# A two-layer sequence trunk on one core: the first MLP's down projection as seven block products, and sums of the last row group on GpSimd

## The chip, the core and the metric

One core of one Trainium2 chip. A core has TensorE (PE, matrix products and the transposes made with them), VectorE (DVE), ScalarE (ACT), GpSimd (POOL) and SyncE (SP, which here only issues transfers). The five have instruction streams of their own and wait for each other through semaphores. The metric is the device time of one execution in microseconds (us); lower is better. All tensors are fp32.

## The reference

```python
def reference(x, mem, ...):                  # x (1, 512, 1024), mem (1, 256, 1024)
    h = x
    for layer in range(2):
        # layer 0: gated DeltaNet mixer; layer 1: Conformer convolution module
        h = h + mixer(rms_norm(h, ...), ...)
        h = h + memory_cross_attention(rms_norm(h, ...), ...)
        h = h + sq_relu_mlp(rms_norm(h, ...), w_up, w_down)
    return rms_norm(h, final_norm)

def sq_relu_mlp(h, w_up, w_down):            # 512x1024 @ 1024x4096, then @ 4096x1024
    return jnp.square(jax.nn.relu(h @ w_up)) @ w_down

def conformer_conv(h, ...):
    u = h @ w_pw1 + b_pw1
    u = u[..., :1024] * jax.nn.sigmoid(u[..., 1024:])
    c = causal_depthwise_conv(u, w_dw) + b_dw          # 31 taps
    return jax.nn.silu(layer_norm(c, ln_g, ln_b)) @ w_pw2 + b_pw2
```

The change concerns the MLP of layer 0. Behind it in the program comes the convolution module of layer 1.

## The kernel before, in words

**Layout and precision.** Activations lie feature-major: a tile holds 128 features by 512 tokens, and the residual `h` is eight such tiles. Each value is split into a rounded part and a rest (`xh` and `xl`, `uh` and `ul`; for weights `wh` and `wl`), and each product is made as three matmuls, high by high, low by high and high by low (`mm3`, L282 to L288). `proj` (L294) runs `mm3` over the eight 128-row pieces k of a contraction of 1024: 24 matmuls of 128x512 for one output tile.

**Weights.** They stream in 128x1024 tiles, in an order planned ahead (`order`, `need`). `wload` (L222) issues a tile's transfer on SP's queue into one of six `raw` buffers; `wsplit` makes `wh` from it (ACT cast, L245) and `wl` (DVE subtraction, recorded at the helper line L69), with three buffers each; `wnext` (L258) hands them to the matmuls in the planned order and keeps loads and splits a few tiles ahead.

**Normalization.** An RMS norm's statistics are collected while its inputs are made. For each finished `h` tile `Norm.add` issues `xh` (ACT L372), `xl` (DVE L72) and a square (ACT L379), and adds the squares up (GpSimd, the last sum on DVE). `Norm.stat`, placed inside the matmuls that consume the tiles, splits the sum (`sqh`, `sql`), sums it over the partitions with matmuls, and takes a root (ACT) and a reciprocal (`rb`, DVE L395). The factor `rb` is multiplied in later, when a product is read out of PSUM.

**The MLP of layer 0** (`mlp`) has four groups of 1024 hidden rows. In the order up 0, up 1, down 0, up 2, down 1, up 3, down 2, down 3 it makes per group eight up tiles and eight down tiles of 24 matmuls each. A down tile is added to the residual by one DVE instruction `h<-dn,h`. In down 3 this instruction also reorders the tokens by phase (t mod 4), as the convolution wants them, and calls `add` of the convolution's norm tile by tile. Ahead of down 3 some work for later is issued (`mid`): the norm of the memory for layer 1's attention (eight `ml` instructions) and loads of the convolution's taps.

**The MLP of layer 1** (`mlp7`) multiplies the 512x1024 activations of a group by its 1024x1024 down weights in the Strassen-Winograd way: seven products of blocks, half the size in each direction, instead of eight (`ORDER7`). Here the activations stand in PE and the weights stream, so the output is token-major. A product is 2 row halves c x 2 weight halves h x 2 k x 3 = 24 matmuls of 512 columns. Sums of weight blocks are needed (T1 to T4): they are made in memory by transfers that add to their destination (`more`, L233, on GpSimd's queue). T1, T2 and T4 are made one after the other in the same two `t` tiles, each after the last use of the one before. The products are collected in `acc` tiles: four for the output blocks (n, m), and `m` and `b` for parts that enter several blocks, each for two row halves c. In the last group `m` and `b` are joined to the blocks by DVE instructions `acc<-acc,acc`, and `final` makes the closing RMS norm out of the token-major rows. At group 0, `turn` transposes the residual into the first four `acc` pairs.

**Behind the first MLP** comes the convolution module. Its first projection (`pw_mm`) makes sixteen tiles in pairs m, one of the value half (`pa`) and one of the gate half (`sg`). The two tiles of the pair m=0 are made one after the other: all eight k of the first, then all of the second, with `norm.stat` inside the second tile's k=1. The taps of the convolution are done by DVE (`ca<-x,prm,ca`, L1192) and partly by GpSimd (`ca<-ca,cvp`), beside the matmuls.

Of the kernel before, what the change touches and what calls it, by code (L numbers as in the profile page):

```python
# [8 lines left out]
F32 = mybir.dt.float32  # L9
F32R = mybir.dt.float32r  # L10
# [27 lines left out]
def tile_trunk(ctx, tc, xT, memT, x_d, mem_d, prm_d, adt_d, bdw_d, tap_d, fin_d, w_ab, w_kq, w_v, w_z, w_dno, w_pw1, w_pw2,  # L38
# [141 lines left out]
    def plan_mlp7(layer):  # L180
        for g in range(4):
            for i in range(4):
                plan(("up", layer, g * 4 + i), w_up[layer, g * 4 + i])
            n, base7["u", g] = len(loads), len(order)
# [4 lines left out]
            for u in range(14):  # L189
                order.append((("dn7", g), u))  # L190
# [12 lines left out]
    plan_mlp(0)  # L203
# [31 lines left out]
    def wsplit():  # L235
# [5 lines left out]
        raw = combos7(1, i, hf) if kind == "dn7" else ws["raw"].pop(need[u])  # L241
# [13 lines left out]
        if kind == "dn7":  # L255
            after7(1, i, hf)
# [13 lines left out]
    def combos7(layer, g, u):  # L270
# [3 lines left out]
        t = ws["raw"].pop(need[u + base7["u", g]])  # L274
# [781 lines left out]
    def mlp(layer, norm, hres, nxt, mid):  # L1056
        xs = norm.xs
        hid = {}
        cur = list(hres)
        st = {"first": []}  # L1060

        def up_ev(g, i, ps):
# [4 lines left out]
            hid.setdefault(g, []).append(split(u, "u"))  # L1067

        for kind, g in MLP_ORDER:
            if (kind, g) == ("dn", 3):  # L1070
                mid()
            for i in range(8):
                w = wnext((kind, layer, g * 4 + i // 2), i % 2)
                ps = psum(kind)
                if kind == "up":
                    proj(w, xs, ps, inside={1: norm.stat} if (g, i) == (0, 1) else None)
                    if g == 0 and i < 2:
                        st["first"].append(ps)
                        if i == 1:
                            for j in range(2):  # L1080
                                up_ev(0, j, st["first"][j])
                    else:
                        up_ev(g, i, ps)
                else:
                    proj(w, hid[g], ps)
                    hn = slot(s="h")
                    if g == 3:
                        tt(dve, by_phase(hn), phased(ps), phased(cur[i]), ALU.add)
                        nxt.add(i, hn)
                    else:  # L1090
                        tt(dve, hn, ps, cur[i], ALU.add)
                    cur[i] = hn
        return cur

# [7 lines left out]
    def by_phase(t):  # L1102
        return t.rearrange("p (s t) -> p s t", s=4)

# [10 lines left out]
    def conformer(norm, hres, nxt):  # L1115
# [409 lines left out]
    h = mlp(0, n2, h, n3, lambda: (mem_gain(1, 0), mem_gain(1, 1), taps(NTAP)))  # L1525
# [5 lines left out]

    def mlp7(layer, norm, hres):
        xs = norm.xs
        acc, first = {}, []
        gt = []

        def turn(i):
            n, m, c = i // 4, i // 2 % 2, i % 2
            ps, a = psum("hT"), slot(s="acc")
            for j in range(4):  # L1540
# [295 lines left out]
```

## Time and profile before

| | |
|---|---|
| time, median of 3 runs | 1486.36 us (1484.01 to 1486.58) |
| the profiled execution: time / span | 1487.96 us / 1486.0 us |
| mean granted TensorE clock | 0.997 of full speed |
| busy: PE, DVE, ACT, POOL | 99%, 66%, 49%, 16% of the span |

Stages of the span, from the timeline: the MLP of layer 0 from 562.70 to 823.80 us, the convolution module from there to 994 us with memory projections and layer 1's cross-attention behind it, the MLP of layer 1 from 1192.81 us to the end.

How to read the profile: an instruction is named by its line, engine, operation and `out<-in` of the program's names. A matmul's duration overlaps the next one's, so that matmuls are counted and priced by the busy time of a stretch. In a timeline row the first number is the start in us from the span's start, the second the duration, and a bracket at the end says how long the engine had been idle before it and what ended that.

### The profile page before, as it was taken

The numbers are of one execution on the slowest core, as the hardware profiler recorded it, in microseconds if no ns is written. First come the engines' busy times: TensorE is split into PE (matmuls) and PEld (weight loads), VectorE is DVE, ScalarE is ACT, GpSimd is POOL, SyncE is SP. The second block draws the span as 40 slices with busy tenths as digits, with TensorE's granted clock in tenths as the row PEclk, the third lists the DMA queues.
The fourth block names the chain that finished last, engine by engine and source line by source line (L and its number), as shares of the span: only waits on it lengthen the run. The fifth ranks groups of instructions, "written<-read, shape, count | busy, mean of one in ns | idle before, by whom it ended". The sixth has DMA issues, their size and how long they took to land.

```text
span 1486.0 us, 19375 instructions
## 1 busy us (share of the span) xinstructions
PE 1472.0 (99%) x7362; PEld 1241.1 (84%) x7362; DVE 986.7 (66%) x1468; ACT 729.0 (49%) x1262; POOL 240.2 (16%) x255
## 2 busy tenths in 40 slices
PE   9999999999999999999999999999999999999997
PEld 7888889988888888888888889988888888888885
DVE  5889888867555543443436699984645766767677
ACT  6766865655444432332314555464444554434344
POOL 1411310103112000000002388302112000000000
PEclk9999999999999999999999999999999999999999
DMA  7232123432213332223224524652203467575634
GB/s 269 93 114 72 58 87 126 142 115 97 73 34 109 99 100 95 91 98 100 99 99 156 174 96 135 192 178 93 86 29 113 114 170 178 140 193 140 186 99 113
DMA packets 55821, 176.63 MB, mean 119 GB/s; under 512 B 6961, under 2 KB 9265, under 8 KB 55729
## 3 DMA queue, kind: packets, MB, share of 16 engines
q1 hardware_dynamic: 50688, 158.10, 32.0%
q0 software_dynamic: 4608, 16.78, 6.6%
q8 instruction: 58, 0.95, 0.3%
q10 hardware_dynamic: 432, 0.52, 0.1%
q14 instruction: 35, 0.28, 0.1%
HBM read 172.49 MB, written 2.10 MB: 117 GB/s over the span
## 4 chain that ended last, share of the span: by engine, by line
PE 94%; DVE 3%; ACT 2%; issue 1%; DMA 1%; POOL 0%; SPq 0%; DVEq 0%
PE up L288 8%; PE up L287 8%; PE up L286 8%; PE dn L287 4%; PE dn L288 4%; PE dn L286 4%; PE dn L1578 3%; PE dn L1579 3%; PE dn L1577 3%; PE pw L288 3%; PE pw L287 3%; PE pw L286 3%; PE h L286 3%; PE h L287 2%; PE h L288 2%; PE xo L287 2%
## 5 line engine op out<-in xcount | busy, mean ns | idle before, releaser
L245 ACT CAST wh<-raw 128x1024 fp32r<-128x1024 f32 x255 | 267.7, 1051 | 498.1 <-PE up L287 133.7
L69 DVE TENSOR_TENSOR wl<-raw,wh 128x1024 fp32r<-128x1024 f32 (+1 forms) x246 | 303.7, 1236 | 93.7 <-ACT wh L245 87.6
L286 PE MATMUL up<-xh,wh 128*128 128x512 f32 x512 | 199.7, 390 | 0.0
L288 PE MATMUL up<-xh,wl 128*128 128x512 f32 x512 | 199.3, 389 | 0.0
L287 PE MATMUL up<-xl,wh 128*128 128x512 f32 x512 | 199.2, 389 | 0.0
L69 POOL TENSOR_TENSOR sq<-sq,sq 128x512 f32<-128x512 f32 x30 | 49.3, 1643 | 468.0 <-ACT sq L379 457.7
L72 DVE SCALAR_TENSOR_TENSOR rl<-up,rb 128x512 f32<-128x512 f32 x64 | 44.2, 691 | 106.0 <-PE up L288 105.9
L287 PEld LDWEIGHTS up<-xl,wh 128*128 128x128 f32 x512 | 96.1, 188 | 19.9
L286 PEld LDWEIGHTS up<-xh,wh 128*128 128x128 f32 x512 | 96.1, 188 | 19.9
L288 PEld LDWEIGHTS up<-xh,wl 128*128 128x128 f32 x512 | 96.1, 188 | 19.9
L286 PE MATMUL dn<-uh,wh 128*128 128x512 f32 x256 | 99.6, 389 | 0.0
L287 PE MATMUL dn<-ul,wh 128*128 128x512 f32 x256 | 99.6, 389 | 0.0
L288 PE MATMUL dn<-uh,wl 128*128 128x512 f32 x256 | 99.6, 389 | 0.0
L69 DVE TENSOR_TENSOR h<-dn,h 128x512 f32<-128x512 f32 x32 | 25.2, 788 | 91.5 <-PE dn L288 91.5
L1192 DVE SCALAR_TENSOR_TENSOR ca<-x,prm,ca 128x512 f32<-128x512 f32 x112 | 82.3, 753 | 3.6 <-ACT ca L1189 1.3
L286 PE MATMUL h<-xh,wh 128*128 128x512 f32 x184 | 73.7, 400 | 0.0
L288 PE MATMUL h<-xh,wl 128*128 128x512 f32 x184 | 71.9, 391 | 0.0
L287 PE MATMUL h<-xl,wh 128*128 128x512 f32 x184 | 71.7, 390 | 0.0
L286 PEld LDWEIGHTS dn<-uh,wh 128*128 128x128 f32 x256 | 48.0, 188 | 10.1
L287 PEld LDWEIGHTS dn<-ul,wh 128*128 128x128 f32 x256 | 48.0, 188 | 9.9
L288 PEld LDWEIGHTS dn<-uh,wl 128*128 128x128 f32 x256 | 48.0, 188 | 9.9
L72 DVE SCALAR_TENSOR_TENSOR cva<-cv,prm,cva 128x512 f32<-128x512 f32 x60 | 48.2, 830 | 11.4 <-POOL cva L69 10.3
(392 smaller groups left out, 3488.5 us busy)
## 6 DMA issues: line engine op xcount, KB each, us to landing
raw<-w_up SPq DMA_DIRECT2D x64, 512.0 KB, 3.5
raw<-w_dn SPq DMA_DIRECT2D x64, 512.0 KB, 3.5
raw<-w_pw SPq DMA_DIRECT2D x24, 512.0 KB, 3.6
t<-w_dn POOLq DMA_DIRECT2D x24, 512.0 KB, 5.6
raw<-w_k SPq DMA_DIRECT2D x16, 512.0 KB, 3.6
raw<-w_vv SPq DMA_DIRECT2D x16, 512.0 KB, 3.9
raw<-w_q SPq DMA_DIRECT2D x16, 512.0 KB, 3.4
raw<-w_o SPq DMA_DIRECT2D x16, 512.0 KB, 3.6
```

The costliest lines, as they stand in the source:

```text
L69: return e.tensor_tensor(out=o, in0=a, in1=b, op=op)
L72: return dve.scalar_tensor_tensor(out=o, in0=a, scalar=s, in1=b, op0=op0, op1=op1)
L245: ins = [act.copy(h, raw)]
L286: pe.matmul(ps, wh, xh, start=first, stop=False)
L287: pe.matmul(ps, wh, xl, start=False, stop=False)
L288: pe.matmul(ps, wl, xh, start=False, stop=last)
L1192: first["tap"] = dve.scalar_tensor_tensor(out=a, in0=src, scalar=w, in1=a, op0=ALU.mult, op1=ALU.add)
L1577: pe.matmul(ps, xh, w[0][:, s], start=opens and k == 0, stop=False, skip_group_check=True)
L1578: pe.matmul(ps, xl, w[0][:, s], start=False, stop=False, skip_group_check=True)
L1579: pe.matmul(ps, xh, w[1][:, s], start=False, stop=k == 3, skip_group_check=True)
```

## The change

- `mlp` and its order are removed; `mlp7` serves both layers. In layer 0 there is no transposed residual at the start: the first product that enters an `acc` tile is copied there by ACT (scale 1 or -1). Per group, up is followed at once by its own seven products: up 0, products 0, up 1, products 1 and so on. `mid` comes ahead of the products of group 3.
- At the end of layer 0's MLP, `outs` transposes the token-major `acc` tiles back: 16 transposes of 128x128 into four PSUM banks for the `h` tiles 0 to 3, inside the last product, and 16 for tiles 4 to 7 behind it. Per tile one DVE instruction adds the residual and reorders by phase, and `add` of the convolution's norm follows.
- `pw_mm` of m=0: k 0 to 3 of the first tile, k 0 to 3 of the second, then k 4 to 7 of each, with `norm.stat` inside the last k=5.
- In the last group of both layers, `m` is joined to block (0,0) and to `b`, and `b` to block (1,0), by GpSimd instead of DVE. Blocks change their places (`BLOCKS7`), so that the two output halves m have changed sides; `turn` and `final` follow that.
- The `acc` tiles of m, b and (1,0) take the convolution's `cv` buffers. Weights of layer 0 are packed as layer 1's were, and `wnext` loads two tiles further ahead in both MLPs.

```diff
-    def plan_mlp(layer):
-        for kind, g in MLP_ORDER:
-            for i in range(4):
-                plan((kind, layer, g * 4 + i), (w_up if kind == "up" else w_dn)[layer, g * 4 + i])
...
-    plan_mlp(0)
+    plan_mlp7(0)
...
-        while ws["load"] <= need[min(i + NRAW + 1 + 2 * (i > base7["u", 0] - 8), len(order) - 1)]:
+        while ws["load"] <= need[min(i + NRAW + 1 + 2 * (order[i][0][0] in ("up", "dn7")), len(order) - 1)]:
...
-    def mlp(layer, norm, hres, nxt, mid):
...
-                    proj(w, hid[g], ps)
-                    hn = slot(s="h")
-                    if g == 3:
-                        tt(dve, by_phase(hn), phased(ps), phased(cur[i]), ALU.add)
-                        nxt.add(i, hn)
-                    else:
-                        tt(dve, hn, ps, cur[i], ALU.add)
...
-    def mlp7(layer, norm, hres):
+    def mlp7(layer, norm, hres, nxt=None, mid=None):
...
+        def acc_tile(key):
+            if key in ACC_CV:
+                return wp.tile([P, 544], F32, tag="cv", name=nm("acc"), bufs=NCV)[:, 0:NT]
+            return slot(s="acc")
...
                     part(left, ws_[h], bank[key][c], c, h, opens)
+                    if layer == 0 and (g, i, c, h) == (3, 6, 1, 0):
+                        outs(range(4))
...
-                    acc[k] = slot(s="acc")
-                    act.copy(acc[k], ps)
+                    acc[k] = acc_tile(key)
+                    act.activation(acc[k], ps, AF.Copy, scale=1.0 if op == ALU.add else -1.0)
                 else:
-                    tt(dve, acc[k], acc[k], ps, op)
+                    tt(e, acc[k], acc[k], ps, op)
...
-                        into((0, 0), c, m)
-                        into(("b",), c, m, ALU.subtract)
+                        into((0, 0), c, m, e=pool)
+                        into(("b",), c, m, ALU.subtract, pool)
...
-                        into((1, 0), c, b, ALU.subtract)
+                        into((1, 0), c, b, ALU.subtract, pool)
...
+        def outs(tiles):
+            todo = [(n, c, i) for n in range(2) for c in range(2) for i in tiles]
+            pss = {i: psum("hT") for i in tiles}
+            for n, c, i in todo:
+                j = 2 * n + c
+                pe.transpose(pss[i][:, j * P:(j + 1) * P], acc[n, 1 - i // 4, c][:, i % 4 * P:i % 4 * P + P], ident)
+            for i in tiles:
+                hn = slot(s="h")
+                tt(dve, by_phase(hn), phased(pss[i]), phased(hres[i]), ALU.add)
+                new[i] = hn
+                nxt.add(i, hn)
...
+            if g == 3 and mid:
+                mid()
...
+        if layer == 0:
+            outs(range(4, 8))
+            return new
...
         def pw_mm(m, hf):
-            st[m, hf] = psum("pw")
-            proj(wnext(("pw1", m), hf), xs, st[m, hf], inside={1: norm.stat} if (m, hf) == (0, 1) else None)
+            w, st[m, hf] = wnext(("pw1", m), hf), psum("pw")
+            if m:
+                return proj(w, xs, st[m, hf])
+            proj(w, xs, st[m, hf], 0, 4)
+            if hf == 0:
+                st["w"] = w
+                return
+            proj(st.pop("w"), xs, st[0, 0], 4, 8)
+            proj(w, xs, st[0, 1], 4, 8, inside={5: norm.stat})
...
-BLOCKS7 = ["11", "21", "12", "22"]
+BLOCKS7 = ["12", "22", "11", "21"]
+ACC_CV = (("m",), ("b",), (1, 0))
-MLP_ORDER = [("up", 0), ("up", 1), ("dn", 0), ("up", 2), ("dn", 1), ("up", 3), ("dn", 2), ("dn", 3)]
```

Lines move by a few: what the profile of before shows at L286 to L288 (`proj`), L372 (`xh`) and L395 (`rb`) stands at L281 to L283, L367 and L390 in the changed kernel; the block products are at L1107 to L1109 and the transposes of `outs` at L1182. The whole PE stream goes from 6589 rows to 6525 in the order listing.

**First place: DVE where layer 0's MLP hands over to the convolution.** `dn` is a down tile's PSUM bank, `h` a finished residual tile, `xl` its low part for the convolution's projection, `wl` a weight tile's low part. Before:

```order
L69 TENSOR_TENSOR h_7142<-dn_7117,h_6798 128x512 [waits PE_49]
L69 TENSOR_TENSOR wl_7154<-raw_7071,wh_7153 128x1024 [waits DMAHW3_49,Activation_49]
L72 SCALAR_TENSOR_TENSOR xl_7146<-h_7142,prm,xh_7144 128x512 [waits Activation_49]
L69 TENSOR_TENSOR h_7182<-dn_7157,h_6831 128x512 [waits PE_49]
L69 TENSOR_TENSOR wl_7194<-raw_7111,wh_7193 128x1024 [waits DMAHW5_49,Activation_49]
L72 SCALAR_TENSOR_TENSOR xl_7186<-h_7182,prm,xh_7184 128x512 [waits Activation_49]
L69 TENSOR_TENSOR h_7222<-dn_7197,h_6864 128x512 [waits PE_49]
L69 TENSOR_TENSOR wl_7252<-raw_7151,wh_7251 128x1024 [waits DMAHW6_49,Activation_49]
L72 SCALAR_TENSOR_TENSOR xl_7226<-h_7222,prm,xh_7224 128x512 [waits Activation_49,Pool_49]
```

After the change, from the low part of the convolution's second weight tile on (`hT` is a bank of transposes; `acc<-acc,dn` reads the last product out):

```order
L69 TENSOR_TENSOR wl_7496<-raw_7354,wh_7495 128x1024 [waits DMAHW4_49,PE_49,Activation_49]
L69 TENSOR_TENSOR h_7458<-hT_7438,h_4558 128x512 [waits PE_49]
L69 TENSOR_TENSOR acc_5472<-acc_5472,dn_7418 128x512 [waits PE_49,Pool_49]
L72 SCALAR_TENSOR_TENSOR xl_7462<-h_7458,prm,xh_7460 128x512 [waits Activation_49]
L69 TENSOR_TENSOR h_7466<-hT_7439,h_4566 128x512
L69 TENSOR_TENSOR acc_5480<-acc_5480,dn_7419 128x512 [waits PE_49,Pool_49]
L69 TENSOR_TENSOR wl_7587<-raw_7380,wh_7586 128x1024 [waits DMAHW6_49,Activation_49]
L72 SCALAR_TENSOR_TENSOR xl_7470<-h_7466,prm,xh_7468 128x512 [waits Activation_49]
L69 TENSOR_TENSOR h_7475<-hT_7440,h_4606 128x512
L72 SCALAR_TENSOR_TENSOR xl_7479<-h_7475,prm,xh_7477 128x512 [waits Activation_49]
L69 TENSOR_TENSOR h_7484<-hT_7441,h_4646 128x512
L72 SCALAR_TENSOR_TENSOR xl_7488<-h_7484,prm,xh_7486 128x512 [waits Activation_49]
```

The residual tiles were spread over the eight down tiles, with one weight split between each two; now all eight stand together behind the last weight splits, `h` and `xl` in turn, four more pairs following the last row shown.

**Second place: PE at the same spot.** Before, the end of the last down tile and the convolution's first matmuls (`pw_7248` is the first tile of pair m=0):

```order
L286 MATMUL dn_7197<-uh_6598,wh_7113 128x512
L287 MATMUL dn_7197<-ul_6600,wh_7113 128x512
L288 MATMUL dn_7197<-uh_6598,wl_7114 128x512
L286 MATMUL pw_7248<-xh_6945,wh_7153 128x512 [waits Activation_49]
L287 MATMUL pw_7248<-xl_6947,wh_7153 128x512
L288 MATMUL pw_7248<-xh_6945,wl_7154 128x512 [waits DVE_49]
L286 MATMUL pw_7248<-xh_6984,wh_7153 128x512
L287 MATMUL pw_7248<-xl_6986,wh_7153 128x512
L288 MATMUL pw_7248<-xh_6984,wl_7154 128x512
L286 MATMUL pw_7248<-xh_7024,wh_7153 128x512
```

After the change, behind the transposes (`pw_7590` and `pw_7607` are the two tiles of pair m=0; from the second k on):

```order
L282 MATMUL pw_7590<-xl_7470,wh_7422 128x512 [waits DVE_49]
L283 MATMUL pw_7590<-xh_7468,wl_7423 128x512
L281 MATMUL pw_7607<-xh_7468,wh_7495 128x512
L282 MATMUL pw_7607<-xl_7470,wh_7495 128x512
L283 MATMUL pw_7607<-xh_7468,wl_7496 128x512
L281 MATMUL pw_7590<-xh_7477,wh_7422 128x512 [waits Activation_49]
L281 MATMUL pw_7607<-xh_7477,wh_7495 128x512
L282 MATMUL pw_7590<-xl_7479,wh_7422 128x512 [waits DVE_49]
L283 MATMUL pw_7590<-xh_7477,wl_7423 128x512
L282 MATMUL pw_7607<-xl_7479,wh_7495 128x512
L283 MATMUL pw_7607<-xh_7477,wl_7496 128x512
L281 MATMUL pw_7590<-xh_7486,wh_7422 128x512 [waits Activation_49]
```

Six matmuls stand for each k, and each k waits for an `xh` of ACT and an `xl` of DVE; before, 24 matmuls of one tile stood here in one piece, k by k, with seven of the eight `h` tiles finished during the down tiles ahead.

**Third place: DVE at the end of layer 1's MLP.** Before, with the joins `acc<-acc,acc` (the row that goes is the seventh):

```order
L69 TENSOR_TENSOR acc_10804<-acc_10804,dn_12579 128x512 [waits PE_49]
L69 TENSOR_TENSOR wl_12763<-t_12439,wh_12762 128x1024 [waits DMASW6_49]
L69 TENSOR_TENSOR acc_10602<-acc_10602,acc_10804 128x512 [waits DVE_49]
L69 TENSOR_TENSOR acc_10481<-acc_10481,acc_10804 128x512
L69 TENSOR_TENSOR y_12757<-acc_10602,gt_12532 128x512 [waits DVE_49]
L78 TENSOR_SCALAR sm_12756<-sm_12753 128x1 [waits Activation_49]
L69 TENSOR_TENSOR acc_10588<-acc_10588,acc_10804 128x512
L69 TENSOR_TENSOR wl_12779<-t_12480,wh_12778 128x1024 [waits DMASW7_49,PE_49]
L69 TENSOR_TENSOR acc_10422<-acc_10422,dn_12616 128x512 [waits PE_49]
```

After:

```order
L69 TENSOR_TENSOR acc_11138<-acc_11138,dn_12913 128x512 [waits PE_49,Pool_49]
L69 TENSOR_TENSOR wl_13097<-t_12773,wh_13096 128x1024 [waits DMASW6_49]
L69 TENSOR_TENSOR acc_10936<-acc_10936,acc_11138 128x512 [waits DVE_49]
L69 TENSOR_TENSOR acc_10815<-acc_10815,acc_11138 128x512
L69 TENSOR_TENSOR y_13091<-acc_10936,gt_12866 128x512 [waits DVE_49]
L78 TENSOR_SCALAR sm_13090<-sm_13087 128x1 [waits Activation_49]
L69 TENSOR_TENSOR wl_13113<-t_12814,wh_13112 128x1024 [waits DMASW7_49,PE_49]
L69 TENSOR_TENSOR acc_10756<-acc_10756,dn_12950 128x512 [waits PE_49]
```

Ahead of the last weight split one join is gone from DVE (the same went a few rows earlier, for the other row half); the row that reads the product out now waits for GpSimd as well.

More of the change, by code (lines that the diff above doesn't have):

```diff
@@ L183, in plan_mlp7 @@
                 plan(("up", layer, g * 4 + i), w_up[layer, g * 4 + i])
-            n, base7["u", g] = len(loads), len(order)
+            n, base7[layer, g] = len(loads), len(order)
             for b, h in LOADS7:
@@ L189, in plan_mlp7 @@
             for u in range(14):
-                order.append((("dn7", g), u))
+                order.append((("dn7", layer, g), u))
                 bh = (ORDER7[u // 2][1], u % 2)
@@ L240, in wsplit @@
         (kind, i, *j), hf = order[u]
-        raw = combos7(1, i, hf) if kind == "dn7" else ws["raw"].pop(need[u])
+        raw = combos7(i, j[0], hf) if kind == "dn7" else ws["raw"].pop(need[u])
         h = wp.tile([P, 1024], F32R, tag="wh", name=nm("wh"), bufs=NW)
@@ L273, in combos7 @@
             return T7[h]
-        t = ws["raw"].pop(need[u + base7["u", g]])
+        t = ws["raw"].pop(need[u + base7[layer, g]])
         if name == "T1":
```

307 lines of the change are left out of this document (141 added, 166 removed).

## The prediction

> **What bounds the kernel now.** I read the busy table first, then the chain of work that ended last, then windows and the timeline around the first MLP.
>
> ```profile
> PE 1472.0 (99%) x7362; PEld 1241.1 (84%) x7362; DVE 986.7 (66%) x1468; ACT 729.0 (49%) x1262; POOL 240.2 (16%) x255
> DVE  5889888867555543443436699984645766767677
> PE 94%; DVE 3%; ACT 2%; issue 1%; DMA 1%; POOL 0%; SPq 0%; DVEq 0%
> ```
>
> PE is busy 99% of the span and carries 94% of the chain: a matmul removed is time removed, unless something else is late in its stage. DVE's slices are the warning. They stand at 3 to 7 tenths in the first MLP (slices 15 to 22) and at 9 in the convolution behind it. The windows of those two stages (per engine busy us and count; then granted clock, DMA share, GB/s) and a run of transposes price the work:
>
> ```profile
> 562.70:823.80 261.10, 261.10 (x1153) 216.22 (x1152) 113.10 (x128) 82.00 (x104) 8.98 (x6) 1.00 0.32 106
> 880.00:920.00 40.00, 40.00 (x217) 34.43 (x216) 39.00 (x57) 23.55 (x48) 36.38 (x24) 1.00 0.29 93
> 1191.58 1.47 PE L1541 MATMUL hT<-ident,h 128*128 128x128 f32 x12
> 1192.81 0.47 PE L1577 MATMUL dn<-wh,ah 128*128 128x512 f32 x1
> 823.82 0.39 PE L286 MATMUL pw<-xh,wh 128*128 128x512 f32 x1
> ```
>
> A 128x512 matmul costs 261.10/1153 = 0.2265 us, not the 0.39 us of its own row, which overlaps the next one's. A transpose costs (1192.81 − 1191.58)/12 = 0.1025 us. PE is full in the whole first MLP, and goes on at 823.82 into the convolution's first matmul without a gap. In the convolution DVE is busy 39.00 of 40.00 us: what comes late there has little room to be caught up.
>
> **The change, part by part.** The sum is made against the profiled execution's own 1487.96 us, 1.60 above the median.
>
> *Matmuls.* Per group 8 × 24 = 192 down matmuls become 7 × 24 = 168: 96 fewer over four groups, 96 × 0.2265 = **−21.7 us**. Transposes back: 32 × 0.1025 = **+3.3 us**. Both lie on PE with nothing beside them.
>
> *The handover into the convolution.* Before, seven of the eight `h` tiles were made during the down tiles, 5.4 us of matmuls apart. Now all eight come at the end, and the order of DVE puts `h` and `xl` in strict turn. What one tile costs there:
>
> ```profile
> 794.04 1.04 DVE L69 TENSOR_TENSOR h<-dn,h 128x512 f32<-128x512 f32 x1
> 795.12 0.72 ACT L372 ACTIVATE xh<-h,prm 128x512 fp32r<-128x512 f32 x1 [1.77 <-DVE h L69]
> 795.88 0.75 DVE L72 SCALAR_TENSOR_TENSOR xl<-h,prm,xh 128x512 fp32r<-128x512 f32 x1 [0.79 <-ACT xh L372]
> 824.02 1.08 DVE L69 TENSOR_TENSOR h<-dn,h 128x512 f32<-128x512 f32 x1 [2.55 <-PE dn L288]
> 825.02 1.21 DVE L69 TENSOR_TENSOR wl<-raw,wh 128x1024 fp32r<-128x1024 f32 x1
> 823.84 1.05 ACT L245 CAST wh<-raw 128x1024 fp32r<-128x1024 f32 x1 [2.89 <-issue]
> 826.82 0.67 DVE L69 TENSOR_TENSOR sq<-sq,sq 128x512 f32<-128x512 f32 x1
> 827.53 0.62 ACT L325 CAST sqh<-sq 128x512 fp32r<-128x512 f32 x1 [1.15 <-DVE sq L69]
> ```
>
> `xl` waits for ACT's `xh` of the same tile, and the next `h` is queued behind that `xl`. So a tile takes h 1.08, wait for `xh` 0.80, `xl` 0.75, less the 0.09 by which DVE rows overlap: 2.54 us. PE eats one k of both first `pw` tiles, six matmuls, in 6 × 0.2265 = 1.36 us. PE will wait for DVE at each k.
>
> Count from Q, where PE has issued the first twelve matmuls of the last product. The cast of the convolution's second weight tile waits for PE to free its buffer at Q: 1.05, and its subtraction 1.21, so DVE is free at Q+2.4; the sixteen transposes were done at Q+1.65. Then in DVE's order, by these rows and 0.65 for an `acc<-acc,dn` (row of the tail, below): h1 to Q+3.45, c=0 of the product read out to 4.1, xl1 to 5.0, h2 to 5.95, c=1 read out to 6.55, a third split to 7.7, xl2 to 8.35, and six more tiles by 2.54 to Q+23.5. PE has four matmuls behind the last `xl`: Q+24.4. Unhindered it would need 32 transposes and 60 matmuls (12 of the product, 48 of the first pair), 3.3 + 13.6 = Q+16.9. That is 7.5 us of waits. The statistics come behind: the last `sq` sum 0.67 ends at Q+24.1, but ACT has a weight cast queued ahead of `sqh`, and that cast waits for PE's last use of its buffer at about Q+24.0. So `sqh` ends at 24.0 + 1.05 + 0.62 = Q+25.6, 1.2 later than PE wants it. Handover: 7.5 + 1.2 = **+8.7 us**. Ends: 0, if DVE and ACT ran this ahead of PE, and 17, if PE's six matmuls for a tile never lay beside the next tile's DVE work (2.4 + 8 × (2.54 + 1.36) − 16.9). I take 8.7, built of rows of the same operations.
>
> *What the convolution keeps of a late start.* Rows of the reciprocal, the evictions, and the ends of DVE's work there:
>
> ```profile
> 832.06 3.35 DVE L395 RECIPROCAL rb<-sd 128x512 f32<-128x512 f32 x1 [0.48 <-ACT sd L393]
> 843.32 1.25 DVE L69 TENSOR_TENSOR wl<-raw,wh 128x1024 fp32r<-128x1024 f32 x1 [4.23 <-ACT wh L245]
> 846.27 0.69 DVE L69 TENSOR_TENSOR sg<-pw,rb 128x512 f32<-128x512 f32 x1 [1.71 <-PE pw L288]
> 851.66 11.84 DVE L1192 SCALAR_TENSOR_TENSOR ca<-x,prm,ca 128x512 f32<-128x512 f32 x15 [1.26 <-ACT ca L1189]
> 993.30 0.69 DVE L69 TENSOR_TENSOR lsl<-la,lsh 128x512 fp32r<-128x512 f32 x1
> 994.27 0.39 PE L287 MATMUL pw<-lsl,wh 128*128 128x512 f32 x1
> ```
>
> Before, the reciprocal ends at 835.41, some 0.4 us behind PE's first pair of tiles (48 matmuls and four of the sums from 823.82: about 835.0). After the change `norm.stat` stands at the pair's end, and by the chain above (sqh Q+25.6, sums, root, 3.35) the reciprocal ends at Q+31.45, 7.0 behind PE. DVE's idle 4.23 and 1.71 us of before take up most of it. PE ends the second pair's last tile at Q+36.95 and the first taps start at Q+44.3 by the same order, 7.4 later; before it was 851.66 − 846.05 = 5.6. DVE lags PE by 1.8 more, then stays full up to its last split at 993.99, which PE wants at 994.27: 0.3 of slack. **+1.5 us.** Ends: 0, if DVE's few idle moments take it up, and 7.0 − 0.4 − 0.3 = 6.3 if none does.
>
> *The last group of layer 0.* The memory's norm now stands ahead of products 3, and its eight `ml` ahead of the split of T1's halves:
>
> ```profile
> 782.50 3.25 DVE L72 SCALAR_TENSOR_TENSOR ml<-mem,prm,mh 128x256 fp32r<-128x256 f32 x8
> ```
>
> That is 0.41 each on DVE, which has 148 us free in this stage; a split of T1 may come some 0.5 late, and T2's added transfer, issued behind that split with nine tap loads in the queues, 0.3. **+0.8 us**; ends 0 and 3.25.
>
> *The tail of layer 1.* Behind PE's last product DVE and ACT close the norm:
>
> ```profile
> 1471.57 0.68 DVE L69 TENSOR_TENSOR acc<-acc,acc 128x512 f32<-128x512 f32 x1
> 1472.17 1.22 DVE L69 TENSOR_TENSOR wl<-t,wh 128x1024 fp32r<-128x1024 f32 x1
> 1473.30 2.06 DVE L69 TENSOR_TENSOR acc<-acc,dn 128x512 f32<-128x512 f32 x3
> 1474.02 0.63 ACT L1648 ACTIVATE fq<-acc 128x512 f32<-128x512 f32 x1 [2.88 <-DVE acc L69]
> ```
>
> DVE is full here (each row starts where the one before ends), and ACT waits 2.88 us for it. Two joins of 0.60 between starts stood ahead of the split at 1472.17 and go to GpSimd: **−1.1 us**. Whether GpSimd's adds slow DVE's is shown in the convolution, by the same DVE instruction with GpSimd adding and with GpSimd idle:
>
> ```profile
> 896.37 1.03 DVE L72 SCALAR_TENSOR_TENSOR glu<-pa,prm,sg 128x512 f32<-128x512 f32 x1
> 896.78 5.90 POOL L69 TENSOR_TENSOR ca<-ca,cvp 128x512 f32<-128x512 f32 x4
> 925.63 0.74 DVE L72 SCALAR_TENSOR_TENSOR glu<-pa,prm,sg 128x512 f32<-128x512 f32 x1
> ```
>
> It takes 1.03 against 0.74, so 0.29 more beside an add of 5.90/4 = 1.47. Two joins per row half that meet DVE work cost a few tenths; ends −1.3 and +1.8 (two adds of 1.47 that hold DVE up in full, less 1.1). The Trainium skill (SBUF — State Buffer, section "Who interferes with whom") speaks against this edit: a DVE instruction with two SBUF inputs contends with a GpSimd instruction that reads SBUF. The trace agrees that there is contention, and its 0.29 us is a slowdown and not a lock for the whole add; with a lock the tail would be +1.8, and the sum 2.9 us higher.
>
> **Sum**: −21.7 + 3.3 + 8.7 + 1.5 + 0.8 − 1.1 = −8.5: 1479.5 in the profiled execution's terms, **1477.9 us** on the median (1486.36 − 8.5).
>
> **Rivals.** (1) *The handover is hidden.* If `h` and `xl` of different tiles overlapped, or PE found other work, the sum is −21.7 + 3.3 − 1.1 = −19.5: 1466.9. Against it: `xl` and the next `h` stand one behind the other in DVE's order, and 2.54 exceeds 1.36. Chance 0.10.
>
> (2) *The convolution keeps its whole delay.* 6.3 in place of 1.5 gives −3.7: 1482.7. For it: DVE at 39.00 of 40.00. Against it: the idle moments of before. Chance 0.17.
>
> (3) *The clock falls in the handover's many short waits.* At half the clock six matmuls take 2.7 us, hardly more than the 2.54 of DVE, so that only what follows pays, some 2.5 us: 1480.4. The one gap in the convolution says this of it:
>
> ```profile
> 955.64 0.39 PE L288 MATMUL K<-mh,wl 128*128 128x256 f32 x1 [1.14 <-POOL wl L69]
> 950.00:975.00 25.00, 23.86 (x149) 21.35 (x148) 24.00 (x35) 14.10 (x25) 5.39 (x4) 1.00 0.73 206
> ```
>
> After 1.14 us of idling the clock stayed at 1.00; a train of some ten waits of 1 to 2 us isn't in the trace. Chance 0.08. The Trainium skill (TensorE: Matmul & The Clock Gate, section "A second HAM failure mode: psum-queue depth-cycling") tells of a clock that swings when PE idles briefly and often, which would be this rival; no run here shows it yet.
>
> (4) *Slower: the added weight sums come late in the first MLP too.* The sums T2 and T4 begin when the split of the sum before has been made and must land before their own split. In layer 1's last group:
>
> ```profile
> 1450.88 0.86 POOL L233 DMA_DIRECT2D t<-w_dn  x1 [1.24 <-DVE wl L69]
> 1457.16 1.05 ACT L245 CAST wh<-t 128x1024 fp32r<-128x1024 f32 x1 [1.80 <-DMA t<-w_dn]
> 1458.24 1.23 DVE L69 TENSOR_TENSOR wl<-t,wh 128x1024 fp32r<-128x1024 f32 x1 [1.63 <-ACT wh L245]
> 1462.20 0.39 PE L1577 MATMUL dn<-wh,sh 128*128 128x512 f32 x1
> DMA to landing us min/median/max: 3.1/5.5/9.3
> ```
>
> That transfer took 6.2 us from issue, and its `wl` was ready at 1459.47 for a matmul at 1462.20: 2.7 us to spare. From a landing of 6.2 + 2.7 = 8.9 us on, PE waits at each of the 16 half tiles (T2 and T4, two halves, four groups); 1 us late at each is +16: −8.5 + 16 = +7.5, 1493.9. For it: the longest was 9.3. Against it: the median 5.5, and the DMA share of 0.32 in the first MLP. Chance 0.07.
>
> That the change doesn't do what it says is out: the order has 64 PE rows fewer, as −96 + 32 asks.
>
> **How the numbers follow.** Forecast 0.55, with its own range 1475 to 1481 (the ends of the small terms); rivals 0.10, 0.17, 0.08, 0.07; 0.03 for something else. The range 1472 to 1484 holds the forecast, (2) and (3), 0.8 together, and leaves out (1) and (4). A difference under 0.2%, 3 us, can't be told from no change by a measurement of this kernel: faster means under 1483.4. That holds for the forecast, (1), (3) and 0.12 of (2)'s 0.17: 0.85. Within: the rest of (2) and 0.02, 0.07. Slower: (4) and 0.01, 0.08.
>
> **What would show it.** The first MLP's PE count falls by 96 with its pitch still 0.2265; transposes stand at some 0.10 each. At the handover, PE's matmuls of `pw` wait for DVE `xl` or ACT `xh` at each k, with `h` rows 2.5 us apart, 8 to 9 us in all; the last `sqh` stands behind a cast. From the first taps on, DVE lags by about 2 us more, and PE waits 1 to 2 us once, near the convolution's end. ACT's last `fq` starts about 1.2 us sooner against PE's end. I am wrong if `h` rows come closer than PE's 1.36 us, if PE waits in the groups for `wl<-t`, or if the granted clock falls behind the handover.

## The result, and the profile after

| | before | after |
|---|---|---|
| median of 12 runs | 1485.51 us (1483.79 to 1487.55) | 1487.43 us (1484.65 to 1490.03) |
| ratio after/before | | 1.0014, 95% interval 1.0005 to 1.0023 |
| profiled execution: time / span | 1487.96 / 1486.0 us | 1486.74 / 1484.7 us |

The prediction said 1477.9 us and 0.85 for faster. The change is slower, by 1.9 us or 0.14%, less than the 0.2% taken as a bound; 1.0 lies outside the interval. The two profiled executions stand the other way round. Their PE streams differ by 1.67 us already where the first MLP's first up matmul starts, after the same program, so all that follows is counted from there. (In the execution of before the granted clock stood at 0.50 for some 3.4 us near its start, which is worth about this difference; in the other it didn't.) First that stretch of before, where the third number from the end is the granted clock, and then the busy table and DVE's slices of the changed kernel:

```profile
8.58:11.90 3.32, 3.32 (x9) 1.96 (x9) 3.23 (x7) 3.10 (x6) 0.00 (x0) 0.50 1.06 396
PE 1461.5 (98%) x7298; PEld 1226.3 (83%) x7298; DVE 1073.3 (72%) x1606; ACT 773.2 (52%) x1330; POOL 287.4 (19%) x299
DVE  6889888867555756767688699985555766767677
```

PE has 64 instructions fewer, as it should; with 96 × 0.2265 − 32 × 0.1025 gone it would be busy for 18.5 us less, but it is only 10.5 less, in part because some matmuls took longer (below). DVE's slices in the first MLP (14 to 22) rose from 3 to 6 tenths to 5 to 8. (The first MLP starts at 475 us; 562.70, which the part ahead gives for it, is where its first down tile starts.) To see where the time stays, I take five matmuls that both programs have. Before, where the prediction hasn't shown them:

```profile
475.17 0.39 PE L286 MATMUL up<-xh,wh 128*128 128x512 f32 x1
836.33 0.39 PE L288 MATMUL pw<-xh,wl 128*128 128x512 f32 x1
1475.62 0.39 PE L1579 MATMUL dn<-wl,ah 128*128 128x512 f32 x1
```

After:

```profile
473.50 0.39 PE L281 MATMUL up<-xh,wh 128*128 128x512 f32 x1
811.05 0.47 PE L281 MATMUL pw<-xh,wh 128*128 128x512 f32 x1
833.45 0.39 PE L283 MATMUL pw<-xh,wl 128*128 128x512 f32 x1
952.77 0.39 PE L283 MATMUL K<-mh,wl 128*128 128x256 f32 x1 [0.82 <-POOL wl L69]
1475.38 0.39 PE L1109 MATMUL dn<-wl,ah 128*128 128x512 f32 x1
```

| stretch | before | after | difference | by the counts | lost |
|---|---|---|---|---|---|
| first MLP: first up to first pw | 348.65 | 337.55 | −11.1 | −21.7 + 28 transposes 2.9 | 7.8 |
| handover: first pw to a pw matmul behind the statistics | 12.51 | 22.40 | +9.9 | 4 transposes 0.4 | 9.5 |
| convolution, to its one gap | 119.31 | 119.32 | 0.0 | 0 | 0.0 |
| from there to the last matmul | 519.98 | 522.61 | +2.6 | 0 | 2.6 |
| last matmul to the end of the span | 10.38 | 9.32 | −1.1 | | −1.1 |

The 18.5 us were there, and 18.8 were lost again: 0.4 us slower in this pair of executions, 1.9 in the medians. Of four places, the prediction had the handover right (9.5 against 8.7); it had put 0.8 us on the last group of the first MLP, which cost 7.8, and a gain of 1.1 on layer 1's tail, which lost 1.6 (the 1.1 is there behind the last matmul, but 2.6 went ahead of it); the fourth, the convolution, was charged 1.5 and cost nothing.

**The last group of layer 0.** PE, DVE and GpSimd of the changed kernel around product 3, which needs the sum T1:

```profile
768.60 3.11 POOL L69 TENSOR_TENSOR acc<-acc,acc 128x512 f32<-128x512 f32 x2 [23.82 <-DVE acc L69]
769.03 1.51 DVE L69 TENSOR_TENSOR s<-u,s 128x256 f32<-128x256 f32 x1
771.84 2.73 POOL L69 TENSOR_TENSOR acc<-acc,acc 128x512 f32<-128x512 f32 x2
771.91 4.93 DVE L72 SCALAR_TENSOR_TENSOR ml<-mem,prm,mh 128x256 fp32r<-128x256 f32 x7
776.76 1.21 DVE L69 TENSOR_TENSOR wl<-t,wh 128x1024 fp32r<-128x1024 f32 x1
778.03 0.79 PE L1109 MATMUL dn<-wl,sh 128*128 128x512 f32 x1 [3.77 <-DVE wl L69]
778.62 0.63 PE L1107 MATMUL dn<-wh,sh 128*128 128x512 f32 x1
779.05 0.63 PE L1108 MATMUL dn<-wh,sl 128*128 128x512 f32 x1
```

The rows stand in order of time. T1's low part `wl` is queued behind seven of the memory's eight `ml` (the row of 4.93: 0.70 each, where before they took 0.41), and those behind an `s` that took 1.51 where the same shape takes 0.42 elsewhere. PE stands for 3.77 us. And then it is slow: the matmuls behind the wait start 0.43 us apart, not 0.2265, for about 15 of them, 3.1 us more. The granted clock says why. The first row is this stretch, the second the handover, the third the slow stretch of a second trace of the same kernel (the first run below):

```profile
777.42:784.25 6.83, 6.22 (x15) 4.87 (x16) 5.64 (x7) 1.04 (x1) 1.75 (x2) 0.50 0.62 94
810.00:834.00 24.00, 18.83 (x72) 10.96 (x71) 18.16 (x20) 12.19 (x19) 7.99 (x6) 1.00 0.23 86
779.97:783.38 3.41, 3.41 (x10) 2.64 (x9) 3.41 (x5) 1.04 (x1) 1.30 (x2) 0.50 0.67 107
```

The clock is at half for 6.83 us here and for 3.41 us in the second trace. Here it falls 0.6 us before PE goes on at 778.03; there it falls 1.0 us after.

**The tail of layer 1**, the same in small:

```profile
1441.16 6.77 POOL L69 TENSOR_TENSOR acc<-acc,acc 128x512 f32<-128x512 f32 x4 [24.51 <-DVE acc L69]
1443.03 0.68 DVE L69 TENSOR_TENSOR acc<-acc,dn 128x512 f32<-128x512 f32 x1
1444.47 4.54 DVE L69 TENSOR_TENSOR wl<-t,wh 128x1024 fp32r<-128x1024 f32 x2
1446.84 0.50 PE L1109 MATMUL dn<-wl,sh 128*128 128x512 f32 x1 [0.47 <-DVE wl L69]
1462.80 6.26 POOL L69 TENSOR_TENSOR acc<-acc,acc 128x512 f32<-128x512 f32 x2 [3.07 <-DVE acc L69]
1463.77 1.28 DVE L69 TENSOR_TENSOR acc<-acc,acc 128x512 f32<-128x512 f32 x2
1467.82 2.38 DVE L69 TENSOR_TENSOR acc<-acc,acc 128x512 f32<-128x512 f32 x2
1472.06 0.50 PE L1109 MATMUL dn<-wl,ah 128*128 128x512 f32 x1 [1.58 <-DVE wl L69]
```

Beside GpSimd's first four adds a weight split takes 4.54/2 = 2.27 us instead of 1.22, while `acc<-acc,dn`, which has one input in PSUM, keeps its 0.68. Beside the last two adds two joins of DVE take 2.38 instead of 1.28. It isn't always DVE that pays: two joins at 1463.77 keep their 1.28, and GpSimd's two adds take 3.13 us each. PE, which waited nowhere here before, waits 0.47 and 1.58.

**The handover**, as forecast:

```profile
816.78 1.05 DVE L69 TENSOR_TENSOR h<-hT,h 128x512 f32<-128x512 f32 x1
818.62 0.75 DVE L72 SCALAR_TENSOR_TENSOR xl<-h,prm,xh 128x512 fp32r<-128x512 f32 x1 [0.79 <-ACT xh L367]
819.29 1.07 DVE L69 TENSOR_TENSOR h<-hT,h 128x512 f32<-128x512 f32 x1
831.73 0.50 PE L386 MATMUL ssq<-sqh,ones_r 128*128 128x512 f32 x1 [1.00 <-ACT sqh L320]
```

An `h` every 2.51 us (2.54 was forecast), each `xl` after a wait of 0.79 for `xh`, and PE waits 1.00 for `sqh` at the end (1.2 forecast).

### The profile page after: what moved, and what is told of

It is laid out like the page before. It is cut to its first block, busy times and chain, and to the rows that moved or that the text cites. A ratio compares the mean times of both kernels' runs of the same rounds, so it can differ in the third digit from the quotient of the medians.

```text
span 1484.7 us, 19622 instructions
## 1 busy us (share of the span) xinstructions
PE 1461.5 (98%) x7298; PEld 1226.3 (83%) x7298; DVE 1073.3 (72%) x1606; ACT 773.2 (52%) x1330; POOL 287.4 (19%) x299
## 5 line engine op out<-in xcount | busy, mean ns | idle before, releaser
L281 PE MATMUL up<-xh,wh 128*128 128x512 f32 x512 | 199.7, 390 | 0.0
L283 PE MATMUL up<-xh,wl 128*128 128x512 f32 x512 | 199.3, 389 | 0.0
L281 PEld LDWEIGHTS up<-xh,wh 128*128 128x128 f32 x512 | 96.1, 188 | 19.9
L283 PEld LDWEIGHTS up<-xh,wl 128*128 128x128 f32 x512 | 96.1, 188 | 19.9
L228 POOL DMA_DIRECT2D t<-w_dn x48 | 42.0, 875 | 354.8 <-DVE wl L69 215.5
L1109 PE MATMUL dn<-wl,ah 128*128 128x512 f32 x256 | 99.9, 390 | 1.7 <-DVE wl L69 1.6
L1107 PE MATMUL dn<-wh,ah 128*128 128x512 f32 x256 | 99.8, 390 | 0.0
L1108 PE MATMUL dn<-wh,al 128*128 128x512 f32 x256 | 99.6, 389 | 0.0
L69 DVE TENSOR_TENSOR wl<-t,wh 128x1024 fp32r<-128x1024 f32 x48 | 61.2, 1278 | 36.1 <-ACT wh L240 36.1
L240 ACT CAST wh<-t 128x1024 fp32r<-128x1024 f32 x48 | 50.6, 1054 | 61.8 <-PE dn L1108 43.7
L281 PE MATMUL h<-xh,wh 128*128 128x512 f32 x184 | 73.7, 400 | 0.0
L283 PE MATMUL h<-xh,wl 128*128 128x512 f32 x184 | 71.9, 391 | 0.0
L69 DVE TENSOR_TENSOR acc<-acc,dn 128x512 f32<-128x512 f32 x96 | 64.6, 682 | 2.6 <-PE dn L1109 1.5
L69 DVE TENSOR_TENSOR al<-u,ah 128x512 fp32r<-128x512 f32 x64 | 44.1, 689 | 20.7 <-ACT ah L320 20.7
```

Source lines behind the costliest of these rows:

```text
L69: return e.tensor_tensor(out=o, in0=a, in1=b, op=op)
L228: nc.gpsimd.dma_start(out=t, in_=a, accum_op=ALU.add)
L240: ins = [act.copy(h, raw)]
L281: pe.matmul(ps, wh, xh, start=first, stop=False)
L283: pe.matmul(ps, wl, xh, start=False, stop=last)
L1107: pe.matmul(ps, xh, w[0][:, s], start=opens and k == 0, stop=False, skip_group_check=True)
```

## The experiments

The theory to test: three places cancel the gain. (A) In layer 0's last group, `ml` and GpSimd's joins make T1's split late, and the long wait is followed by slow matmuls. (B) At the handover the strict turn of `h` and `xl` sets PE's pace. (C) GpSimd's joins cost DVE more than they save it, in layer 1's tail too. The first four kernels ran on one chip against a median of before of 1485.29 us, the next four against 1485.06.

**The changed kernel again.**

> The changed kernel once more, for a second trace of it. Theory: what cancels the gain sits at fixed places, so the trace shows again one wait of 3 to 4 us for T1's low part in layer 0's last group, then some 14 matmuls at 0.43 us instead of 0.2265 (3 us), some 8.5 us of short waits at the handover and 2 us of waits for weight splits in layer 1's last group; time 0 to +3 us against before. Rival: the wait and the slow matmuls are an accident of the one execution; then the wait is under 1 us or the matmuls behind it keep their 0.2265, and the time falls to about -5 us.

It took 1488.00 us, ratio 1.0011 (1.0002 to 1.0020). The wait for T1 is 3.77 us again, followed by 8 slow matmuls (1.6 us); the handover's rows are the same to a tenth; layer 1's last group waits 0.47 and 2.21. The places are fixed; the number of slow matmuls isn't: the clock stood at half for 3.41 us, not 6.83.

**The joins back on DVE**, in both layers:

```diff
-                        into((0, 0), c, m, e=pool)
-                        into(("b",), c, m, ALU.subtract, pool)
+                        into((0, 0), c, m)
+                        into(("b",), c, m, ALU.subtract)
...
-                        into((1, 0), c, b, ALU.subtract, pool)
+                        into((1, 0), c, b, ALU.subtract)
```

> The changed kernel with the joins of the last groups back on DVE. Theory (GpSimd's adds hold up DVE instructions that read two tiles of SBUF, as long as DVE's own joins would take, or longer): in layer 0's last group DVE gets four joins of 0.60 back (2.4 us) and loses 3.6 us of stretched rows (s 0.42 to 1.51, ml 0.41 to 0.70), so T1's wait falls from 3.8 to about 2.5 us; if the slow matmuls come of that wait's length they go too. Layer 1's tail goes back to what before had, 1.5 us less. Together 3 to 6 us faster than the changed kernel, -2 to -4 against before. Rival (GpSimd's adds are nearly free for DVE, the wait is the ml instructions' alone): 2.4 us more on DVE ahead of T1, wait 6 us, the tail as before the change; 2 us slower than the changed kernel.

It took 1481.86 us, ratio 0.9976 (0.9966 to 0.9986): 6 us faster than the changed kernel. DVE has more work and is earlier. Its rows there, and PE's:

```profile
770.09 0.41 DVE L69 TENSOR_TENSOR s<-u,s 128x256 f32<-128x256 f32 x1
774.19 1.66 DVE L72 SCALAR_TENSOR_TENSOR ml<-mem,prm,mh 128x256 fp32r<-128x256 f32 x4
776.10 0.50 PE L1107 MATMUL dn<-wh,ah 128*128 128x512 f32 x1 [0.78 <-ACT wh L240]
778.25 0.50 PE L1109 MATMUL dn<-wl,sh 128*128 128x512 f32 x1 [0.95 <-DVE wl L69]
```

`s` is back at 0.41 and `ml` at 0.42. The wait of 3.77 became two of 0.78 and 0.95: T1's low part is ready 0.8 us sooner, counted from the first up matmul, and in this kernel's order matmuls of the next product stand inside the wait. No slow matmuls follow. Since the order changed too, this run by itself doesn't say how much of the wait the adds had made; the rows of `s` and `ml` do, some 3.6 us shorter together. Later in the group PE waits 0.52 for T2 and 0.95 for T4, and nowhere in layer 1's last group. The theory of (C) holds; the rival would have made the kernel slower.

**The memory's norm one group earlier**, joins still on GpSimd:

```diff
         for g in range(4):
             ops, us = [{} for _ in range(4)], []
+            if g == 3 and mid:
+                mid()
...
-            if g == 3 and mid:
-                mid()
```

> The changed kernel with the memory's norm (eight mh and ml) and the tap loads issued one group earlier. Theory (the eight ml, 4.9 us on DVE beside GpSimd's adds, and the eight mh on ACT stand ahead of T1's split): T1's wait of 3.8 us falls under 0.5 and the matmuls behind it run at 0.2265; 6 to 7 us faster than the changed kernel. Rival (the wait is the joins' and would come anyway, or goes over to group 2's products): a wait of 2 to 4 us stays or appears in group 2, time within 1.5 us of the changed kernel.

It took 1483.49 us, ratio 0.9986 (0.9977 to 0.9995): 4.5 us faster than the changed kernel, less than the theory's 6 to 7. T1's wait falls to 0.48, with no slow matmuls behind it; the `ml` rows lie between the splits of group 2 and nothing waits there. What keeps it from 6 us are waits of 0.53 for T2 and 1.57 for T4 in the last group:

```profile
786.71 1.05 ACT L240 CAST wh<-t 128x1024 fp32r<-128x1024 f32 x1 [3.96 <-DMA t<-w_dn]
793.59 4.33 DVE L69 TENSOR_TENSOR acc<-acc,acc 128x512 f32<-128x512 f32 x4
```

T2's is a wait for the sum in memory: the cast waits 3.96 us for the transfer, and the split for the cast (the same holds for the 0.52 of the run above). Ahead of T4's split stand four joins of DVE beside two on GpSimd, 4.33 us for four where all six take 3.69 with the joins on DVE. `ml` and joins together made the long wait; either one taken away breaks it.

**`h` one tile ahead of `xl`** at the handover:

```diff
                 new[i] = hn
-                nxt.add(i, hn)
+                if i % 4:
+                    nxt.add(i - 1, new[i - 1])
+            nxt.add(tiles[-1], new[tiles[-1]])
```

> The changed kernel with the next tile's h made ahead of each tile's xl at the handover, so that DVE does not stand while ACT makes xh. Theory (the strict turn of h and xl, 2.54 us a tile, sets PE's waits): a tile takes 1.08 + 0.75 - 0.2 = 1.66 us, six tiles give back 5.3 us, the waits at the handover fall from 8.5 to about 3.5 us, and the end comes 4 to 5 us sooner. Rival 1 (ACT's chain of casts and squares, or the weight splits, sets the pace): waits stay at 7 us or more. Rival 2 (the convolution is bound by DVE, which starts its taps as late as before): the waits fall, but PE waits as much more later in the convolution, and the time stays.

It took 1484.03 us, ratio 0.9990 (0.9982 to 0.9999): 4 us faster than the changed kernel. DVE and PE there:

```profile
819.05 0.77 DVE L72 SCALAR_TENSOR_TENSOR xl<-h,prm,xh 128x512 fp32r<-128x512 f32 x1
819.72 1.11 DVE L69 TENSOR_TENSOR h<-hT,h 128x512 f32<-128x512 f32 x1
820.72 0.81 DVE L72 SCALAR_TENSOR_TENSOR xl<-h,prm,xh 128x512 fp32r<-128x512 f32 x1
814.72 0.50 PE L282 MATMUL pw<-xl,wh 128*128 128x512 f32 x1 [1.67 <-DVE xl L72]
827.18 0.50 PE L386 MATMUL ssq<-sqh,ones_r 128*128 128x512 f32 x1 [1.00 <-ACT sqh L320]
```

A tile takes 820.72 − 819.05 = 1.67 us, as reckoned. From the first `pw` matmul (809.59) to `ssq` it is now 17.6 us, where it was 831.73 − 811.05 = 20.7: 3.1 back, less than the 5.3 of the sum, since the second `xl` still stands behind a read-out and a weight split (PE waits 1.67 for it) and `sqh` is no earlier. The gain is kept through the convolution: rival 2 is out. (B) holds.

**Only GpSimd's joins in layer 1, on the kernel before.** The edit gives `into` the choice of an engine and sends its three calls of the last group to GpSimd, nothing else.

> The kernel before, with nothing changed but the last group's joins in layer 1, which go to GpSimd. Theory (GpSimd's adds hold DVE up longer than the joins would take on it): the rows that stand beside the adds are stretched (wl 1.2 to 2.3 us, acc<-acc,acc 0.64 to 1.2), PE waits twice for wl, some 2.5 us together, and the last chain behind PE is 1.1 us shorter: 1 to 2 us slower than before. Rival (the recorded prediction's step): 1.1 us faster, without waits of PE.

It took 1486.88 us, ratio 1.0012 (1.0003 to 1.0021): 1.8 us slower than before, 0.4 to 3.1 by the interval. PE's two waits are those of the changed kernel:

```profile
1447.09 0.50 PE L1579 MATMUL dn<-wl,sh 128*128 128x512 f32 x1 [0.47 <-DVE wl L69]
1472.17 0.50 PE L1579 MATMUL dn<-wl,ah 128*128 128x512 f32 x1 [1.43 <-DVE wl L69]
```

This is the recorded step by itself, and it goes the other way.

**The first two tiles of the convolution one after the other again.**

```diff
-            if m:
-                return proj(w, xs, st[m, hf])
-            proj(w, xs, st[m, hf], 0, 4)
...
+            proj(w, xs, st[m, hf], inside={1: norm.stat} if (m, hf) == (0, 1) else None)
```

> The changed kernel with the convolution's first two tiles one after the other again (24 matmuls each). Theory (DVE's turn of 2.54 us a tile sets the pace, PE has then only 0.68 us of work per tile beside it): the last xl comes at the same time, and behind it stand 24 matmuls more (5.4 us) in place of the three of its k; the wait of 1.2 us for sqh falls into them: about 4 us slower than the changed kernel. Rival (the pace is PE's or the order does not matter): within 1 us.

It took 1487.43 us, ratio 1.0014 (1.0005 to 1.0023). This told nothing of the question: the order of instructions came out as in the changed kernel, except for the numbers of buffers, so in either spelling the two tiles' matmuls stand k by k beside each other. The edit of `pw_mm` thus does nothing here, and the run is a third trace of the changed kernel (waits of 3.77 for T1 and 2.19 in the tail).

**All three edits**: joins on DVE, the memory's norm earlier, `h` ahead.

> All three edits of the first call together: joins on DVE, the memory's norm a group earlier, h ahead of xl. Theory (three separate places: layer 0's last group, its handover, layer 1's tail): in the last group two waits of 1.7 us together are left of 7.8 us, the handover gives back 3.1, the tail 1.6: 10 to 11 us faster than the changed kernel, 8 against before. Rival (the same time counted several times, since PE is then bound by something else, DVE in the convolution above all): 6 to 7 us faster than the changed kernel.

It took 1474.36 us, ratio 0.9929 (0.9915 to 0.9942): 10.7 us faster than before. Against the run above, which has the changed kernel's order and ran on the same chip (1487.43), that is 13.1. It is near the 14.6 that the edits gave one by one on the other chip (6.1, 4.5 and 4.0), and more than the 10 to 11 expected, since the two waits that the theory left in the last group didn't come. Between the first up and the first `pw` it takes 329.9 us, 0.4 more than 1442 matmuls of 0.2265 and 28 transposes of 0.1025 need. With both `ml` and GpSimd's adds gone, PE waits for none of T1, T2 and T4:

```profile
773.09 1.22 DVE L69 TENSOR_TENSOR wl<-t,wh 128x1024 fp32r<-128x1024 f32 x1
774.23 1.29 DVE L69 TENSOR_TENSOR acc<-acc,acc 128x512 f32<-128x512 f32 x2
775.43 1.22 DVE L69 TENSOR_TENSOR wl<-t,wh 128x1024 fp32r<-128x1024 f32 x1
822.62 0.50 PE L386 MATMUL ssq<-sqh,ones_r 128*128 128x512 f32 x1 [0.99 <-ACT sqh L320]
```

T1's first split ends 299.2 us behind the first up matmul, where it ended 304.5 behind it. **With b's joins behind T4's split**, besides:

```diff
-                            into((1, 0), c, b, ALU.subtract)
+                        if layer:
+                            into((1, 0), c, b, ALU.subtract)
+                        else:
+                            later.append((c, b))
```

> As the three edits together, and in layer 0 the joins of b into block (1,0) moved behind the split of T4. Theory (four of six joins of 0.60 stand ahead of T4's split, and PE waits about 1 us for it): 1 us less than the three edits give, the wait for T4's low part under 0.3 us. Rival (the wait is for T4's sum in memory): no change against the three edits.

It took 1474.96 us, ratio 0.9932 (0.9919 to 0.9944), the same. Neither theory was tested: the wait that it was to remove wasn't there any more.

**Splits repeated, to make PE wait**, in the version with all three edits:

```diff
+        for _ in range(STALL.get((kind, i, *j, hf), 0)):
+            tt(dve, lo, raw, h.bitcast(F32), ALU.subtract)
```

> The version with all three edits, and in it six weight splits of the MLPs' up tiles repeated 5 to 10 times more on DVE (1.14 us each; the repeats write the same values again), so that PE waits for them in a stretch that has no other waits. A split has about 6 us of cover, so the waits should come out as a ladder from 0 to some 6 us. Theory (the run of 0.43 us matmuls in the changed kernel comes of the length of the wait ahead of it): short waits are followed by matmuls at 0.2265, and from some length between 2.4 and 3.8 us on a run of 8 to 14 matmuls at 0.43 follows each. Rival (the slow run has another cause at that place, the burst of transfers or GpSimd's adds): no slow matmuls behind any of the waits.

It was run once, in 1485.13 us; this time isn't used. The ladder didn't come out: of the six places, four made PE wait, for 0.73 (three times) and 2.35 us. The one longer wait has slow matmuls behind it, far from `ml` and GpSimd's adds:

```profile
1161.74 0.80 PE L285 MATMUL up<-xh,wl 128*128 128x512 f32 x1 [2.35 <-DVE wl L69]
1162.34 0.63 PE L283 MATMUL up<-xh,wh 128*128 128x512 f32 x1
1162.76 0.63 PE L284 MATMUL up<-xl,wh 128*128 128x512 f32 x1
1161.70:1165.10 3.40, 3.36 (x8) 2.68 (x9) 3.40 (x5) 1.74 (x3) 0.00 (x0) 0.50 0.57 195
```

The granted clock is 0.50 here too. So the slow matmuls go with the wait and need neither `ml` nor GpSimd. The length of the wait alone doesn't say from when on they come; the last section has more on it.

## Why the prediction was wrong

- **Matmuls and transposes: right.** −21.7 + 3.3, which the version with all three edits shows with 0.4 us to spare in the first MLP.
- **The handover: right in mechanism and size**, 9.5 against 8.7, with 2.51 us per tile against 2.54 and 1.00 us for `sqh` against 1.2.
- **The convolution: the lag was right, its price wrong.** The first taps start 1.3 us earlier than before while PE is 2.9 earlier, a lag of 1.6 (1.8 forecast). The sum charged 1.5 at the end, since it counted only the last 0.3 us of slack. The table's 0.0 shows that nothing was left to pay, and DVE caught up on the way: its last low part `lsl` starts at 990.42, 2.9 earlier than before (993.30), as PE does. (Before, PE's first pair holds two matmuls of the sums, not the four that the prediction counted; this touches only the upper end of the term.)

```profile
850.36 11.84 DVE L1336 SCALAR_TENSOR_TENSOR ca<-x,prm,ca 128x512 f32<-128x512 f32 x15 [1.26 <-ACT ca L1333]
990.42 0.69 DVE L69 TENSOR_TENSOR lsl<-la,lsh 128x512 fp32r<-128x512 f32 x1
```

- **The last group of layer 0: the step that failed most**, "0.41 each on DVE, which has 148 us free in this stage; a split of T1 may come some 0.5 late". The cost was 7.8 us, beyond the bound of 3.25: some 3.9 for the wait (start to start), 3.1 for the matmuls at half the clock, the rest small. Free time of a whole stage says nothing of a burst: a half tile of block products lasts 12 × 0.2265 = 2.7 us, half of an up or down tile's 5.4, so a split has half the cover. The burst wasn't 3.25 alone either: the joins of layer 0, new work that had no counterpart before, weren't priced at all, though they stand at the same spot and stretched `ml` and `s`. The clock, too: the rival that let it fall put this at the handover, where it stayed at 1.00 through the many short waits; it fell to 0.50 at the one long wait. (The prediction read DVE's slices 15 to 22 as 3 to 7 tenths; the line has 3 to 6.)
- **The tail of layer 1: the wrong end was taken.** "Two joins per row half that meet DVE work cost a few tenths; ends −1.3 and +1.8" was taken as −1.1, and came out at +1.6 in the trace, +1.8 by itself. The row that this was sized from, `glu` at 1.03 against 0.74, begins at 896.37, and GpSimd's adds at 896.78: it overlaps them for 0.6 us only and isn't the price of an add. Here four adds stretch `s` by 1.09, the next `s` by 0.5 and two splits by 2.1: 3.7 us, 0.9 per add, where a join on DVE takes 0.60. The rule of the Trainium skill (SBUF — State Buffer, section "Who interferes with whom") that a DVE instruction with two SBUF inputs contends with a GpSimd instruction that reads SBUF is what the runs show, with these numbers; my reading of the trace against it was the mistake. This step by itself, on the kernel before, is 1.8 us of loss, but its interval leaves 0.4 to 3.1.
- **The late sums (rival 4)** didn't happen in the changed kernel: PE waits for no transfer in the first MLP, only for a split queued late on DVE. With a shorter wait for T1, the sum T2 came late once, by 0.5 us (two runs).

Counted place by place the misses are +7.0 in layer 0's last group, +2.7 in the tail, +0.8 at the handover and −1.5 in the convolution, together +9.0, which leads from −8.5 to the traces' +0.4 but for rounding.

## What to carry to other kernels

When the work of an engine on the critical path is cut, price what its helpers must do in the shorter time at the burst, not over the stage: list what is queued ahead of the one instruction that the path needs next, here seven `ml` ahead of T1's `wl`, drawn out by four joins on GpSimd beside them. Work moved to a second engine to relieve a first one is only relief if the two don't hold each other up: look at one row of the first engine that lies wholly beside the second's, and compare it with the same row alone. A change that moves nothing in the sum can hold a gain: undo its parts one by one (here −10.7 us came out of a change of +1.9).

## What the runs showed of the hardware

- An add of two 128x512 tiles on GpSimd cost DVE some 0.9 us of its own time (`s` 0.42 to 1.51, `wl` 1.22 to 2.27), and took GpSimd itself 1.4 to 3.1 us, by what DVE did beside it. A DVE row with one input in PSUM (`acc<-acc,dn`, 0.68) wasn't stretched.
- After a long wait of PE the granted clock can fall to half, and matmuls run at 0.43 us instead of 0.2265. After 3.77 us this came each time (four traces), for 8 to 15 matmuls, 1.6 to 3.1 us lost. After 2.19 to 2.35 us it came in three traces (7 to 8 matmuls) and not in a fourth (2.21 us). No wait up to 1.67 us had it behind, nor did the handover's eight waits of 0.30 to 1.00 us in a row (1.00 in the window of 810 to 834).
- Why one wait of 2.2 us has slow matmuls behind it and another hasn't, and how many, the traces tell in part. Their record of the granted clock changes only in steps of 3.413 us: each stretch is a whole number of them (3.41, 6.83, 310.61 = 91 steps, 771.41 = 226). I divided all eleven traces into these steps and took PE's idle time in each. Behind the first 12 us, 18 steps at full clock had 1.97 us or more (seven inside the programs, eleven at their ends), and half clock followed each of them; it followed no other, and the most idle of those had 1.89. At half clock inside the programs, steps with 0.27 us or less were followed by full clock, the two with 0.61 and 0.99 by another step at half. So what a wait costs depends on how it falls on the steps, too. The two closest are these, the first from the run with the edit of `pw_mm` undone (wait 2.19, half clock behind it), the second from the changed kernel again (wait 2.21, full clock behind it); the number after the length is PE's busy time:

```profile
1469.80:1473.21 3.41, 1.44 (x6) 1.23 (x7) 3.25 (x7) 1.11 (x5) 0.00 (x0) 1.00 0.00 0
1469.47:1472.88 3.41, 1.52 (x7) 0.92 (x5) 3.41 (x5) 0.72 (x2) 0.73 (x1) 1.00 0.00 0
```

These are bounds from the traces of this kernel alone, and no run tested them; near the start of before half clock followed a step with 1.25 us of idle time, so idle time isn't the whole of it.
